# One tile of constants made 32 bytes longer in a two-layer hybrid decoder trunk

## Chip, cores and metric

The kernel runs on one core of a Trainium2 chip. The metric is the device time of one execution in microseconds (us), the median of several runs; lower is better.

## The reference

Two layers of a post-norm decoder trunk over 256 tokens of width 1024, all in float32. For each layer:

```
proj = x @ w_in                       # 1024 -> 12800, cut into the parts below
y_A  = B * conv3_causal(C * h)        # short gated convolution, width 1024
y_B  = dilated attention, 3 groups of 8 heads of 64 (window, dilation) = (128,1), (512,4), (2048,16),
       rotary on q and k, the groups merged by their softmax denominators
y_C  = gelu(u) * (tril(W_s) @ LN(gelu(v)) + b)      # per chunk of 128 tokens, width 1024
m = sig(g_A)*(y_A P_A) + sig(g_B)*(y_B P_B) + sig(g_C)*(y_C P_C)
x = LN(alpha*x + m W_o)
x = LN(alpha*x + (silu(x W_gate) * (x W_up)) W_down)   # inner width 2816
```

## The kernel before

Every large product is made of three matmuls. A float32 matrix is split into a high and a low part of 12 bits each (`split`, lines 177 to 180: ScalarE copies the high part, VectorE subtracts it), kept in the type fp32r, 4 bytes an element, and h.T h' + h.T l' + l.T h' is summed in PSUM. Weights come from HBM in panels (`Panel`, line 144), three of them in flight (tile `raw`, 8 KB a partition), and are split in pieces of 512 columns just before TensorE needs them. `tick` (line 209) puts this work of the other engines, and attention, between runs of matmuls; it goes by a planned TensorE time that `spend` adds up (327 ns for three matmuls of 256 columns, 1.28 ns a column for three of 512).

There are two forms of the large product:

- `feat` (line 250, matmuls on lines 246 to 248): features on partitions. Weights of 128 columns stand, 256 tokens move. The moving tile is xh or xl (the two parts of x, with features on partitions), or the parts of a branch: yah, yal (convolution), ybh, ybl (attention), ych, ycl (gMLP). A panel has 48 matmuls (24 for the attention branch).
- `toks` (line 263, matmuls on lines 266 to 268): tokens on partitions. 128 tokens of x (xh, xl), of the hidden units of the feed-forward (hh, hl) or of the summed branches (mh, ml) stand, and the weights move, 512 columns at a time, or 256 in the first two blocks of the feed-forward.

In the names of the trace the moving tile comes first: `acc<-xh,wh` moves xh against standing weights wh, `acc<-wh,hh` moves weights against standing hidden units.

The rest of TensorE's work is small: transposes by an identity that is kept in the constants `con` (lines 296, 442, 451, 612, 804), the scores and the products with values of attention (lines 591 to 595, 622), and the gMLP's spatial product (line 701, plain fp32; one such matmul is two instructions).

Places in the SBUF, per partition. A tile begins at the next multiple of 32 bytes behind the one before. The constants come first: `con` (line 130) has 1282 columns of 4 bytes, 5128 bytes, and begins at byte 16512, a multiple of 64. Behind it, in this order: xt at 21664, xh at 29856, xl at 38048, cos, sin, two small constants, the three `raw` tiles from 48352 in steps of 8192, and the 72 slots (`flat`, line 110) from 72928 in steps of 2048, which hold split weights, branches, hidden units, queries, keys and everything else of that size. Small tiles follow. All of xt, xh, xl, raw and the slots so begin at 32 past a multiple of 64; xh and xl at 32 past a multiple of 128, the slots at 96 past one. Rows of 1024 or 2048 bytes within them are what a matmul reads, and begin in the same manner.

Of the kernel before, what the change touches and what calls it, by code (L numbers as in the profile page):

```python
# [11 lines left out]
F32 = mybir.dt.float32  # L12
# [26 lines left out]

# Weights: columns split at a time, panels loaded ahead.  # L40
PIECE = 512
RAW = 3
# Slots of 2 KB a partition; those that weights leave to others.
NS = 72
SPARE = 8
# TensorE time between two turns of the other engines' work, ns.
TICK = 1300
# Pieces of weights to have ready for splits to wait behind a layer norm.
CALM = 8
# [3 lines left out]
WAIT = 5  # L53
# Steps of attention a turn.
PACE = 0.5

# Column layout of the constants.
C_ID = 0
# [4 lines left out]
C_N = C_M + 2 * 512  # L63

TWO_PI = 2 * math.pi
# Pieces, of few bits each, of 2*pi and of (2**20, 2**9)/(2*pi) less its whole turns.
PI_PARTS = (6.283203125, -1.7818063497543335e-05, 2.4308402678243113e-10)
# [5 lines left out]
def constants():  # L73
    """Identity, masks and rotary frequencies: they depend on shapes alone."""
    c = np.zeros((128, C_N), np.float32)
    i = np.arange(128)
    c[:, C_ID:C_ID + 128] = np.eye(128)
    # Attention keeps tokens ordered by their residue mod 2, in two tiles: a tile of queries sees
    # all keys of the first group, and of the dilated ones only the keys of its own tile.
    tok = np.arange(S).reshape(128, 2).T.reshape(-1)  # L80
    for t in range(2):
        own = slice(t * 128, (t + 1) * 128)
        m = C_M + t * 512
        for g, (keys, n) in enumerate(((slice(0, S), S), (own, 128), (own, 128))):
            dist = tok[own, None] - tok[None, keys]
            ok = (dist >= 0) & (dist % DIL[g] == 0) & (dist <= 128 * DIL[g])
            c[:, m:m + n] = np.where(ok, 0.0, NEG)
            m += n
    c[:, C_TRI:C_TRI + 128] = i[:, None] <= i[None, :]
    c[:, C_FREQ] = (10000.0 ** (-(i % 32) / 32.0)).astype(np.float32)  # L90
    c[:, C_SGN] = np.where(i % 64 < 32, -1.0, 1.0)
    return c
# [3 lines left out]
def trunk(ctx: ExitStack, tc: tile.TileContext, a, out):  # L96
# [32 lines left out]

    con = cp.tile([128, C_N], F32, name="con")  # L130
    ident = con[:, C_ID:C_ID + 128]
# [7 lines left out]

    # ---------------------------------------------------------------- weights  # L140
    cnt = dict(loaded=0, split=0, made=0, front=0, hold=4, calm=0)
    panels = []

    class Panel:
        """Weights [kc * 128, nw], kept as 12-bit parts h + l in pieces of 512 columns."""

# [22 lines left out]
        def at(self, k, c, n):  # L169
            """Columns c..c+n of row block k, both parts."""  # L170
            i, o = divmod(k * self.nw + c, PIECE)
            while len(self.h) <= i:
                piece()
            cnt["front"] = max(cnt["front"], self.first + i + 1)
            return self.h[i][:, o:o + n], self.l[i][:, o:o + n]

    def split(h, l, src):
        """h + l = src, both of them of 12 bits."""
        nc.scalar.activation(h, src, AF.Copy)  # L179
        V.tensor_tensor(l, src, h.bitcast(F32), op=OP.subtract)  # L180
# [15 lines left out]
    def used(n=1):  # L196
        """Pieces of weights done with."""
        free(2 * n)
# [6 lines left out]
    def soon(n, f):  # L205
        """f at the n-th turn from here."""
        timed.append((clock[1] + n, f))

    def tick():
        """Work of other engines, and attention, between runs of matmuls."""  # L210
        clock[1] += 1
        loaded = False
        while timed and timed[0][0] <= clock[1]:
            timed.pop(0)[1]()
            loaded = True
        if hooks:
            hooks.popleft()()
        clock[2] += PACE if slow else 0
        if clock[2] >= 1:
            clock[2] -= 1  # L220
            slow.popleft()()
            loaded = True
        lead = cnt["made"] - cnt["front"]
        if clock[1] <= cnt["calm"] and lead >= CALM:
            n = 0
        elif lead < LOW:
            n = 2
        elif loaded:
            n = 1 if lead < HIGH else 0
        elif slow:  # L230
            n = 2 if lead < TOP else 1
        else:
            n = 1 + (clock[1] % 2 and not hooks)
        for _ in range(n):
            if cnt["made"] != cnt["hold"] and cnt["split"] < len(panels) and live[0] + 2 + SPARE <= NS:
                piece()
# [7 lines left out]
    def mm3(o, hl, rhs_h, rhs_l, first, last):  # L244
        """o (+)= h.T @ (h' + l') + l.T @ h'."""
        nc.tensor.matmul(o, lhsT=hl[0], rhs=rhs_h, start=first, stop=False)  # L246
        nc.tensor.matmul(o, lhsT=hl[0], rhs=rhs_l, start=False, stop=False)  # L247
        nc.tensor.matmul(o, lhsT=hl[1], rhs=rhs_h, start=False, stop=last)  # L248

    def feat(p, rhs):  # L250
        """Features on partitions: (panel).T @ activations, a bank for two blocks."""
        ps = acc()
# [10 lines left out]
    def toks(ps, lhs, p, k, c, n, first, last):  # L263
        """Tokens on partitions: activations.T @ panel, one row block into one bank."""
        h, l = p.at(k, c, n)
# [9 lines left out]
    def by_residue(x):  # L275
        """Tokens (innermost) in the order of attention."""
        if len(x.shape) == 2:
# [14 lines left out]
    def to_features(t, q):  # L292
        """Half of x of a token tile, transposed and split."""
        ps = trp()
# [4 lines left out]

    # ---------------------------------------------------------------- layer norm  # L300
    def load_gb(g, b, dma=nc.gpsimd.dma_start):
# [8 lines left out]
    def norm(src, stats, gb, done=lambda h: None):  # L310
        """Layer norm in place of rows of 1024: src the halves, stats their bn_stats."""
        mv = small("mv", (128, 2))
# [6 lines left out]
        V.reciprocal(sd[:, 1:2], sd[:, 0:1])  # L319
        # One Newton step: y (1.5 - 0.5 (v + eps) y y).  # L320
        V.scalar_tensor_tensor(sd[:, 2:3], sd[:, 1:2], sd[:, 3:4], sd[:, 1:2], op0=OP.mult, op1=OP.mult)
# [13 lines left out]
    def resid(t, h, ps):  # L335
        """x = alpha x + (a branch), and the statistics of the half row."""
        V.scalar_tensor_tensor(x_half(t, h), x_half(t, h), ALPHA, ps, op0=OP.mult, op1=OP.add)  # L337
# [3 lines left out]

    # ---------------------------------------------------------------- rotary tables
    rope = {}
# [5 lines left out]
    def rope_tables():  # L349
        """sin and cos of position * frequency, exactly reduced for any position."""  # L350
        pos = rope["pos"]
# [55 lines left out]

    # ---------------------------------------------------------------- one layer
    def layer(L, steps):
# [9 lines left out]

        # Small parameters of the layer.  # L420
        def params():
# [38 lines left out]

        # gMLP gate: gelu and layer norm, tokens on partitions.
        v_t = {}
# [45 lines left out]
        c = OFF_V  # L508
        steps.append(([win(c + nh * 512, 512, 4, k0) for nh in range(2) for k0 in (0, 4)], gv))

        # Attention values, tokens on partitions.
        va = {}
# [17 lines left out]

        # Queries and keys, rotated; features on partitions.
        qk = {}

        def stack(hf, w, r):
            """12-bit parts of the first group: a product over 128 rows gives both cross terms of a head."""
            up, dn = slice(0, 64), slice(64, 128)
# [4 lines left out]
            for i, (own, other) in enumerate(((up, dn), (dn, up))):  # L541
                s = slot("stack", F32R)
                if w:
                    # k: low part at the head's own rows, high part at the others.
                    nc.scalar.activation(s[other], r[own], AF.Copy)
                    V.tensor_tensor(s[own], r[own], kh[own].bitcast(F32), op=OP.subtract)
                else:
                    # q: high part at the head's own rows, low part at the others.
                    nc.scalar.activation(s[own], r[own], AF.Copy)
# [29 lines left out]
        def attend(hf):  # L579
            """Queue attention of four heads behind the next panels."""  # L580
            state = {}
# [74 lines left out]

        # Short convolution.
        ya = {}
# [31 lines left out]

        # gMLP: u * (tril(W_s) v + b).
        yc = {}
# [28 lines left out]

        # Gates, branch products, their sum.
        mT = {}
# [36 lines left out]

        # x = LN(alpha x + m W_o)
        def wo(P):
# [16 lines left out]

        # Feed-forward.  # L780
        hT = {}

        def ff_first(P):
            """The first two blocks: tokens on partitions, a token tile at a time."""
            for j in range(2):
# [109 lines left out]

    # TensorE's clock rises with use: keep it busy until the data arrives.
    idle = small("idle", (128, 64), 1)
# [45 lines left out]
```

## Time and profile before

| | us |
|---|---|
| median of 3 runs | 1177.97 (1177.68 to 1178.27) |
| span of the profiled execution | 1174.9 |
| TensorE busy in it | 1164.0 |
| VectorE busy | 789.3 |
| ScalarE busy | 622.8 |

The profiled execution has no time of its own beside its span, from the first to the last instruction; the runs' times contain some work around it. How to read it: each engine has its own queue, so an engine's busy time counts only where nothing else ends later. Matmuls are pipelined: the next begins before the one before has ended, so the duration of one (some 280 ns for 256 columns) is longer than the distance from its start to that of the next, and the sum of durations exceeds the busy time. A timeline gives each matmul's start, and so this distance.

### The profile page before, as it was taken

What the parts mean: (1) busy time and instruction counts of PE and PEld (TensorE: products, weight loads), DVE (VectorE), ACT (ScalarE), POOL (GpSimd) and SP (SyncE); (2) the same over time, 40 slices, a digit from 0 to 9 for tenths busy, and PEclk for the clock granted to TensorE, in tenths of its full rate; (3) what the DMA queues carried; (4) which work ended last, traced back from release to release, by engine and by line L of the source; (5) the groups of instructions that cost most, each with busy time, mean ns of one, the idle gap of its engine ahead of it and who ended that gap; (6) DMA issues with size and microseconds to landing.
All of it is one profiled execution on the core that took longest, in us unless ns stands there. A gap on an engine that the chain in (4) does not pass through costs nothing.

```text
span 1174.9 us, 21651 instructions
## 1 busy us (share of the span) xinstructions
PE 1164.0 (99%) x8884; PEld 1101.0 (94%) x8884; DVE 789.3 (67%) x1426; ACT 622.8 (53%) x1126; POOL 14.2 (1%) x29
## 2 busy tenths in 40 slices
PE   9999999999999999999999999999999999999997
PEld 7899999999999899998888999999999999999985
DVE  6978886666755777556496677766676567764534
ACT  6666554676544466445185454546755444654530
POOL 0000000000000000000100000000000000000000
PEclk9999999999999999999999999999999999999999
DMA  9588554435857378448367664453566583774530
GB/s 343 202 258 251 171 167 146 142 126 197 265 178 235 111 228 281 171 146 317 113 215 250 181 188 135 151 172 109 177 216 204 194 251 108 253 234 160 176 111 36
DMA packets 180695, 222.41 MB, mean 189 GB/s; under 512 B 5456, under 2 KB 154228, under 8 KB 180596
## 3 DMA queue, kind: packets, MB, share of 16 engines
q1 hardware_dynamic: 178500, 214.66, 55.7%
q0 software_dynamic: 1952, 6.31, 1.9%
q8 instruction: 69, 1.13, 0.4%
q14 instruction: 30, 0.25, 0.1%
q10 hardware_dynamic: 144, 0.07, 0.0%
HBM read 213.67 MB, written 1.05 MB: 183 GB/s over the span
## 4 chain that ended last, share of the span: by engine, by line
PE 98%; DVE 1%; DMA 0%; ACT 0%; SPq 0%; issue 0%
PE acc L246 22%; PE acc L247 21%; PE acc L248 21%; PE acc L267 9%; PE acc L268 9%; PE acc L266 9%; PE acc L622 1%; PE trp L595 1%; PE trp L612 1%; PE trp L592 1%; PE acc L701 1%; PE trp L296 0%; DMA raw<-in_w_in 0%; PE trp L591 0%; PE trp L804 0%; PE trp L442 0%
## 5 line engine op out<-in xcount | busy, mean ns | idle before, releaser
L180 DVE TENSOR_TENSOR wl<-raw,wh 128x512 fp32r<-128x512 f32 x776 | 490.9, 686 | 179.8 <-ACT wh L179 171.2
L246 PE MATMUL acc<-xh,wh 128*128 128x256 f32 x1856 | 523.1, 282 | 0.0
L247 PE MATMUL acc<-xl,wh 128*128 128x256 f32 x1856 | 514.9, 277 | 0.0
L248 PE MATMUL acc<-xh,wl 128*128 128x256 f32 x1856 | 514.8, 277 | 0.0
L179 ACT ACTIVATE wh<-raw 128x512 fp32r<-128x512 f32 x776 | 432.1, 622 | 69.7 <-DMA raw<-in_w_in 26.5
L246 PEld LDWEIGHTS acc<-xh,wh 128*128 128x128 f32 x1856 | 348.8, 188 | 6.0 <-issue 2.1
L248 PEld LDWEIGHTS acc<-xh,wl 128*128 128x128 f32 x1856 | 349.8, 188 | 0.0
L247 PEld LDWEIGHTS acc<-xl,wh 128*128 128x128 f32 x1856 | 348.8, 188 | 0.1
L266 PE MATMUL acc<-wh,xh 128*128 128x512 f32 (+1 forms) x288 | 100.4, 349 | 0.3 <-ACT xh L179 0.3
L267 PE MATMUL acc<-wl,xh 128*128 128x512 f32 (+1 forms) x288 | 98.8, 343 | 0.2 <-DVE wl L180 0.2
L268 PE MATMUL acc<-wh,xl 128*128 128x512 f32 (+1 forms) x288 | 98.8, 343 | 0.0
L266 PE MATMUL acc<-wh,hh 128*128 128x512 f32 x176 | 68.6, 390 | 0.0
L268 PE MATMUL acc<-wh,hl 128*128 128x512 f32 x176 | 68.5, 389 | 0.0
L267 PE MATMUL acc<-wl,hh 128*128 128x512 f32 x176 | 68.5, 389 | 0.0
L266 PEld LDWEIGHTS acc<-wh,xh 128*128 128x128 f32 x288 | 54.7, 190 | 7.2 <-ACT wh L179 0.5
L267 PEld LDWEIGHTS acc<-wl,xh 128*128 128x128 f32 x288 | 54.8, 190 | 6.8 <-DVE wl L180 0.5
L268 PEld LDWEIGHTS acc<-wh,xl 128*128 128x128 f32 x288 | 54.7, 190 | 6.6 <-DVE xl L180 0.4
L599 ACT ACTIVATE p<-p,ml 128x512 f32<-128x512 f32 x32 | 23.3, 728 | 61.3 <-DVE ml L598 56.3
L179 ACT ACTIVATE hh<-hs 128x512 fp32r<-128x512 f32 x18 | 11.4, 634 | 64.3 <-DVE hs L823 64.3
L316 ACT ACTIVATE sd<-mv,eps 128x1 f32<-128x1 f32 x12 | 3.6, 298 | 72.4 <-DVE mv L313 72.4
L337 DVE SCALAR_TENSOR_TENSOR xt<-xt,acc 128x512 f32<-128x512 f32 x16 | 11.0, 685 | 44.5 <-PE acc L268 44.5
L268 PEld LDWEIGHTS acc<-wh,hl 128*128 128x128 f32 x176 | 33.0, 188 | 6.8
(148 smaller groups left out, 1329.1 us busy)
## 6 DMA issues: line engine op xcount, KB each, us to landing
raw<-in_w_in SPq DMA_DIRECT2D x99, 1024.0 KB, 5.3
raw<-in_w_gate SPq DMA_DIRECT2D x22, 1024.0 KB, 5.8
raw<-in_w_up SPq DMA_DIRECT2D x22, 1024.0 KB, 5.2
raw<-in_w_down SPq DMA_DIRECT2D x22, 1024.0 KB, 4.8
raw<-in_p_a SPq DMA_DIRECT2D x8, 1024.0 KB, 5.3
raw<-in_p_c SPq DMA_DIRECT2D x8, 1024.0 KB, 5.1
raw<-in_w_o SPq DMA_DIRECT2D x8, 1024.0 KB, 5.7
sw<-qk SPq DMA_DIRECT2D x96, 64.0 KB, 3.0
```

Of the source, the lines that this page charges most:

```text
L179: nc.scalar.activation(h, src, AF.Copy)
L180: V.tensor_tensor(l, src, h.bitcast(F32), op=OP.subtract)
L246: nc.tensor.matmul(o, lhsT=hl[0], rhs=rhs_h, start=first, stop=False)
L247: nc.tensor.matmul(o, lhsT=hl[0], rhs=rhs_l, start=False, stop=False)
L248: nc.tensor.matmul(o, lhsT=hl[1], rhs=rhs_h, start=False, stop=last)
L266: nc.tensor.matmul(ps, lhsT=lhs[0], rhs=h, start=first, stop=False)
L267: nc.tensor.matmul(ps, lhsT=lhs[0], rhs=l, start=False, stop=False)
L268: nc.tensor.matmul(ps, lhsT=lhs[1], rhs=h, start=False, stop=last)
L592: nc.tensor.matmul(ps[:, c], lhsT=q[d, b, own], rhs=qk[hf, "kh"][d, b, keys], start=False, stop=True)
L595: nc.tensor.matmul(ps[:, c], lhsT=q[d, b, own], rhs=k[d, b, keys], start=True, stop=True)
L599: nc.scalar.activation(p, p, AF.Exp, bias=ml[:, 0:1], scale=-1.0, accum_out=ml[:, 1:2])
L612: nc.tensor.transpose(ps[:, i * 128:(i + 1) * 128], p[:, i * 128:(i + 1) * 128], ident)
```

## The change

The tile of the constants is allocated with 8 more columns, 32 bytes, of which nothing is used. Its place and the columns that are read stay. Every tile behind it begins 32 bytes later: xh at 29888, xl at 38080, the slots from 72960. The distances between those tiles stay. Apart from that the change takes comments and descriptions out of the file and leaves empty lines in their place, so that line numbers are the same; the hunks that do only this are left out here.

```diff
@@ -127,7 +127,7 @@
     def trp():
         return pt.tile([128, 512], F32, tag="trp", name="trp")
 
-    con = cp.tile([128, C_N], F32, name="con")
+    con = cp.tile([128, C_N + 8], F32, name="con")[:, :C_N]
     ident = con[:, C_ID:C_ID + 128]
     xt = cp.tile([128, 2, D], F32, name="xt")
     xh = cp.tile([128, 8, S], F32R, name="xh")
```

## Rows read from the trace of the kernel before

**Rows 1.** The page: span; busy time; TensorE's granted clock; the last chain.
```profile
span 1174.9 us, 21651 instructions
...
PE 1164.0 (99%) x8884; PEld 1101.0 (94%) x8884; DVE 789.3 (67%) x1426; ACT 622.8 (53%) x1126; POOL 14.2 (1%) x29
...
PEclk9999999999999999999999999999999999999999
...
PE 98%; DVE 1%; DMA 0%; ACT 0%; SPq 0%; issue 0%
```

**Rows 2.** Waits of TensorE, longest first: total us, times, longest us.
```profile
PE trp L905 <- DVE half_pi L900: 1.0, 1, 1.0
```

**Rows 3.** TensorE's groups by line and shape: count, busy us, mean ns of one.
```profile
L246 PE MATMUL acc<-xh,wh 128*128 128x256 f32 x1856 | 523.1, 282 | 0.0
...
L266 PE MATMUL acc<-wh,hh 128*128 128x512 f32 x176 | 68.6, 390 | 0.0
...
L266 PE MATMUL acc<-wh,xh 128*128 128x512 f32 x160 | 63.8, 399 | 0.3 <-ACT xh L179 0.3
...
L266 PE MATMUL acc<-wh,xh 128*128 128x256 f32 x128 | 36.5, 286 | 0.0
L246 PE MATMUL acc<-yah,wh 128*128 128x256 f32 x128 | 36.5, 285 | 0.0
...
L266 PE MATMUL acc<-wh,mh 128*128 128x512 f32 x64 | 25.3, 395 | 0.0
...
L612 PE MATMUL trp<-con,p 128*128 128x128 f32 x128 | 19.2, 272 | 0.0
L246 PE MATMUL acc<-ybh,wh 128*128 128x256 f32 x64 | 18.3, 286 | 0.0
...
L701 PE MATMUL acc<-wsT,gv 128*128 128x128 f32 x64 | 8.4, 274 | 0.0
```

**Rows 4.** Timeline of TensorE, feed-forward of layer 0: start us, us; first and last of 831.
```profile
430.79 0.28 PE L246 MATMUL acc<-xh,wh 128*128 128x256 f32 x1
...
524.86 0.28 PE L248 MATMUL acc<-xh,wl 128*128 128x256 f32 x1
```

**Rows 5.** The same timeline, feed-forward of layer 1: first and last of 828.
```profile
1008.64 0.28 PE L246 MATMUL acc<-xh,wh 128*128 128x256 f32 x1
...
1106.04 0.28 PE L248 MATMUL acc<-xh,wl 128*128 128x256 f32 x1
```

**Rows 6.** The same timeline, branch products of layer 0: first and last of 111.
```profile
305.29 0.28 PE L246 MATMUL acc<-yah,wh 128*128 128x256 f32 x1
...
318.49 0.28 PE L248 MATMUL acc<-ych,wl 128*128 128x256 f32 x1
```

**Rows 7.** The same timeline, down projection of layer 1: first and last of 261.
```profile
1106.15 0.39 PE L266 MATMUL acc<-wh,hh 128*128 128x512 f32 x1
...
1165.09 0.39 PE L268 MATMUL acc<-wh,hl 128*128 128x512 f32 x1
```

**Rows 8.** The same timeline, first products of layer 0: two stretches, 75 and 141.
```profile
13.39 0.39 PE L266 MATMUL acc<-wh,xh 128*128 128x512 f32 x1
...
30.33 0.39 PE L268 MATMUL acc<-wh,xl 128*128 128x512 f32 x1
...
31.25 0.40 PE L266 MATMUL acc<-wh,xh 128*128 128x512 f32 x1
...
63.91 0.40 PE L268 MATMUL acc<-wh,xl 128*128 128x512 f32 x1
```

**Rows 9.** The same timeline: a transpose of attention, and the gMLP's spatial product.
```profile
130.00 0.60 PE L612 MATMUL trp<-con,p 128*128 128x128 f32 x4
...
219.54 1.05 PE L701 MATMUL acc<-wsT,gv 128*128 128x128 f32 x8
```

**Rows 10.** The page: groups of the weights' split on VectorE and ScalarE.
```profile
L180 DVE TENSOR_TENSOR wl<-raw,wh 128x512 fp32r<-128x512 f32 x776 | 490.9, 686 | 179.8 <-ACT wh L179 171.2
...
L179 ACT ACTIVATE wh<-raw 128x512 fp32r<-128x512 f32 x776 | 432.1, 622 | 69.7 <-DMA raw<-in_w_in 26.5
```

## The prediction

> **What bounds the kernel now.** I read the page first, for the engine that sets the end: TensorE is busy for 99% of the span, its granted clock is full in every slice, and the chain that ended last is 98% TensorE and 1% VectorE [rows 1]. Second, the waits of TensorE: the longest in the whole trace is 1.0 us, at the start [rows 2]. So no load, split or wait sets the time; only the rate at which TensorE passes from one matmul to the next does. Third, therefore, the timeline of TensorE, where the reader should look at the distance between the starts of neighbouring matmuls (the pitch), not at the duration of one, since durations overlap. I take a long unbroken stretch, subtract its first start from its last and divide by the number of steps.
>
> - xh or xl moving (256 columns), weights standing: 430.79 to 524.86 us holds 831 matmuls, so 94.07 us / 830 = 113.3 ns [rows 4]. The same code in the second layer, 1008.64 to 1106.04 us, 828 matmuls: 97.40 / 827 = 117.8 ns [rows 5].
> - a branch (slots) moving, 256 columns, weights standing: 305.29 to 318.49 us, 111 matmuls: 13.20 / 110 = 120.0 ns [rows 6].
> - weights moving, 512 columns, hidden units (slots) standing: 1106.15 to 1165.09 us, 261 matmuls: 58.94 / 260 = 226.7 ns [rows 7].
> - weights moving, 512 columns, x standing: 13.39 to 30.33 us, 75 matmuls: 16.94 / 74 = 228.9 ns; then 31.25 to 63.91 us, 141 matmuls: 32.66 / 140 = 233.3 ns [rows 8].
> - the identity in con moving (a transpose, 128 columns, which take as long as 256 of the others): four in 0.60 us, of which the last takes 0.272 us, so 0.328 / 3 = 109 ns [rows 9, 3]. A plain fp32 product of 128 columns out of a slot: eight in 1.05 us, (1.05 - 0.274) / 7 = 111 ns [rows 9, 3].
>
> At 2.4 GHz a column takes 0.4167 ns, so 256 take 106.7 and 512 take 213.3 ns. Every fp32r pitch is over that, and by an odd kind of amount. In units of 16 columns (6.67 ns) the pitches are 17.0, 17.67 (53 per three matmuls), 18.0, 34.0, 34.33 and 35.0, where 16 and 32 would be enough. Sixteen columns of 4 bytes are 64 bytes. That is how a reader looks that fetches its moving operand in aligned pieces of 64 bytes, at the speed at which it uses them up: a row of 1024 bytes that begins 32 past a multiple of 64 touches 17 pieces instead of 16. The one tile that begins at a multiple of 64, con, is the one with 109 ns and no whole piece on top. This is an inference: con's matmuls are transposes, so they differ from the others in more than the place. The fp32 product out of a slot, at 111 ns, reads half as many bytes in that time and is hardly held up either, which fits a limit on bytes fetched.
>
> **The change part by part.** It adds no instruction, no DMA and no wait, and moves none: only addresses change, by 32 bytes, for all tiles behind con. Unchanged are the distances between these tiles. Comments fall away, which costs nothing.
>
> Counts are of [rows 3]: a group of L246 stands for three lines, L246 to L248, a group of L266 for L266 to L268.
>
> Forecast: one piece of 64 bytes less in each fp32r matmul, 6.67 ns, but none faster than con's 109 ns.
> 1. xh moving: 3 x 1856 = 5568. The stretch of rows 5 (828) at 6.67 ns: 5.5 us. The other 4740 I count at 113.3, though shorter stretches of 117.8 lie among them: 113.3 to 109 is 4.3 ns, 20.6 us. Together 26.1.
> 2. branches moving: 3 x (128 + 128 + 64) = 960 (ych has as many as yah), 6.67 ns: 6.4.
> 3. weights moving, slots standing: 3 x (176 + 64) = 720: 4.8.
> 4. weights moving in 512 columns, x standing: 3 x 160 = 480: 3.2.
> 5. weights moving in 256 columns, x standing: 3 x 128 = 384. They have no pitch of their own here; taken as 113.3, 4.3 ns: 1.7.
> Sum 42.2 us.
>
> Lower end: all of them go to con's rate, columns plus 109 - 106.7 = 2.3 ns, so 109 and an estimate of 215.7 ns. Then 1: 20.6 + 828 x 8.8 = 27.9; 2: 960 x 11.0 = 10.6; 3: 720 x 11.0 = 7.9; 4: a third at 13.2, two thirds at 17.6: 7.7; 5: 1.7. Sum 55.8 us. I take the single piece, since what is over it (18 for 17, 34 for 33, 35 for 33) differs between pairs of operands that are misplaced alike, so something other than the place makes it.
>
> First what the rows show: 113.3 to 120 ns for 256 columns and 226.7 to 233.3 for 512. Beside it stands the Trainium skill, TensorE: Matmul & The Clock Gate, section "Wait — 56ns, not 53.3ns?": warm matmuls start N/2.4 ns plus about 2.5 ns apart, which would be 109.2 and 215.8. The trace agrees for con's transposes (109) and not for the fp32r matmuls; if the change brought them there, the sum would be that of the lower end.
>
> **What covers it.** A panel of 48 matmuls falls from 5.4 to 5.2 us. In it VectorE needs 4 x 686 ns and ScalarE 4 x 622 ns for its splits [rows 10], 2.7 and 2.5 us; so neither becomes the bound, and I cost the shift at nothing there. If alignment alters VectorE's own operations, what shows is the 1% of the chain that it holds, 12 us: even 5% of them, either way, is 0.6 us. DMAs write to shifted rows too; no DMA stands in the chain (0%) [rows 1], so a faster one brings nothing, and a slower one would have to use up the panels that are loaded ahead. Zero, with 0.6 us of room.
>
> **The rivals.**
> - *Only the tiles in slots gain* (terms 2 to 5, 16.1 us: 1161.9). In bytes modulo 128, xh begins at 32 and slots at 96; after the change at 64 and 0. If whole pieces are fetched from a multiple of 128 on, the counts would be (32 + 1024)/64, up to 17, for xh, (96 + 1024)/64, up to 18, for the branches and (96 + 2048)/64, up to 34, for the hidden units: exactly rows 4, 6 and 7. Then xh at 64 stays at 17. Against it: weights moving with x standing begin at 96 too, and take 34.33 and 35 [rows 8].
> - *No change* (1178.0): the extra 16 columns come of how the weight load and the moving stream take turns, which hangs on the distance between their tiles, and that stays. For it: rows 4, 6 and 8 differ at the same misplacement modulo 64, and one code has two pitches [rows 4, 5]. Against it: what is left over is always a multiple of a third of a piece or a whole one, and con has nearly none. Also here: a reader with pieces of 32 bytes or less, for which these tiles are in place already. The Trainium skill, SBUF — State Buffer, section "Specifications (TRN2)", speaks for this one: it gives cachelines of 16 bytes, so the shift would do nothing. No row here shows pieces of 16 bytes; the steps seen are of 64.
> - *Slower*: the two pitches of rows 4 and 5 are two ways in which the same two streams lock, and a stretch keeps the one that it fell into. A shift of 32 bytes can set which one it falls into. If the slower one takes hold of the other 4740 matmuls of xh, that is 4740 x (117.8 - 113.3) = 21 us: 1199. It decides from the point where more than about half of them are caught and the shift saves no piece.
> - That the change does not do what it says: con is 5128 bytes, kept in 5152 as places go in steps of 32; 5160 need 5184, so the tiles do move. I give this nothing.
>
> **How the numbers follow.** The profiled execution has a span of 1174.9 us [rows 1], 3.1 below the median of 1177.97; I keep that distance. Forecast: 1177.97 - 42.2 = 1135.8 (span 1132.7), chance 0.33. To con's rate: 1122.2, 0.20. Only slots: 1161.9, 0.10. No change: 1178, 0.22. Slower: 1199, 0.15. So faster by over 0.2% has 0.63, within 0.2% (2.4 us, about what a measurement of this kernel can tell from no change) 0.22, slower 0.15. The range goes from 1119, the lower end with some room for the shorter stretches that I counted as fast, to 1181, which takes in no change; it leaves out the slower case, 0.15.
>
> **What would show it.** Right: con's transposes stay at 109 ns; the xh stretch of 430 to 525 us shows 109 to 111 ns; the branches 113.3 or less, the hidden units 220 or less; instruction counts, the clock and the shares of the chain stay. If xh stays at 113.3 while the branches go to 113.3 or less, it is the reader from multiples of 128. If every pitch of the first list stands as it was, the pieces are no matter of the place. I am wrong as well if pitches fall but TensorE begins to wait for splits: then the waits of TensorE, 1.0 us at most now, would grow.

## The result, and the profile after

The changed kernel takes 1183.93 us against 1178.12 of the kernel before on the same chip: 1.0051 times as long, 95% interval 1.0036 to 1.0065. It is slower by 5.8 us. The page of the kernel after, in the parts that [rows 1] shows of before:

```profile
span 1181.1 us, 21651 instructions
...
PE 1170.6 (99%) x8884; PEld 1107.5 (94%) x8884; DVE 789.6 (67%) x1426; ACT 621.7 (53%) x1126; POOL 14.2 (1%) x29
...
PEclk9999999999999999999999999999999999999999
...
PE 99%; DVE 1%; DMA 0%; SPq 0%; issue 0%; ACT 0%; DVEq 0%
```

TensorE is still the bound, and the whole loss is in its busy time (1164.0 to 1170.6 us) at a full clock, with the same number of instructions. The waits of TensorE, longest first, have not grown beside [rows 2]:

```profile
PE trp L905 <- DVE half_pi L900: 1.0, 1, 1.0
```

So the pitch has to be read again. The timeline of TensorE in the kernel after (start us, us, line), first and last matmul of the feed-forward of layer 0 (834 matmuls, [rows 4]), of layer 1 (828, [rows 5]), of a block of branch products (111, [rows 6]) and of the down projection (261, [rows 7]):

```profile
430.80 0.28 PE L246 MATMUL acc<-xh,wh 128*128 128x256 f32 x1
...
528.91 0.28 PE L248 MATMUL acc<-xh,wl 128*128 128x256 f32 x1
...
1014.85 0.28 PE L246 MATMUL acc<-xh,wh 128*128 128x256 f32 x1
...
1112.25 0.28 PE L248 MATMUL acc<-xh,wl 128*128 128x256 f32 x1
...
305.46 0.28 PE L246 MATMUL acc<-yah,wh 128*128 128x256 f32 x1
...
318.66 0.28 PE L248 MATMUL acc<-ych,wl 128*128 128x256 f32 x1
...
1112.37 0.39 PE L266 MATMUL acc<-wh,hh 128*128 128x512 f32 x1
...
1171.30 0.39 PE L268 MATMUL acc<-wh,hl 128*128 128x512 f32 x1
```

Layer 1: 97.40 / 827 = 117.8 ns; branches: 13.20 / 110 = 120.0; hidden units: 58.93 / 260 = 226.7. All three are to the digit what they were. But layer 0: 98.11 / 833 = 117.8 ns, where [rows 4] had 113.3. A second long stretch did the same: the first rotated panels of layer 1. First and last of 441 matmuls, in the kernel before (49.87 / 440 = 113.3 ns):

```profile
643.53 0.28 PE L246 MATMUL acc<-xh,wh 128*128 128x256 f32 x1
...
693.40 0.28 PE L248 MATMUL acc<-xh,wl 128*128 128x256 f32 x1
```

and in the kernel after (51.82 / 440 = 117.8 ns):

```profile
647.74 0.28 PE L246 MATMUL acc<-xh,wh 128*128 128x256 f32 x1
...
699.56 0.28 PE L248 MATMUL acc<-xh,wl 128*128 128x256 f32 x1
```

No pitch here is new. xh moving against weights has two steady pitches, 340.0 and 353.3 ns for three matmuls (a triple: lines 246, 247 and 248 once), and the change moved stretches from the one to the other. I counted triples of such matmuls with no other work between them, from the starts in the two traces: before, 1,255 at 340 ns, the pitch of [rows 4], and 423 at 353.3 ns, that of [rows 5]; after, 823 and 857 (the stretches above hold 278, 276 and 147 of them). The 434 more at 13.33 ns make 5.79 us, and 5.81 were lost between the medians. The two profiled spans lie 6.2 us apart; 0.3 us of that is in the 384 matmuls that move 256 weight columns past x, 45.8 us from each start to the next before and 46.1 after, because more of them stand 118 ns apart.

The rows that the prediction leaned on as the one aligned tile, con, and as the plain fp32 product out of a slot ([rows 9]), after:

```profile
130.11 0.60 PE L612 MATMUL trp<-con,p 128*128 128x128 f32 x4
...
219.67 1.05 PE L701 MATMUL acc<-wsT,gv 128*128 128x128 f32 x8
```

Both are as long as before, though the slot now begins at a multiple of 64 like con. So it was not their place that set con's transposes apart. They are transposes of 128 columns in plain float32; which of these makes their 109 ns is not shown.

### The profile page after: what moved, and what is told of

It reads as the page before. It is cut to its first block, busy times and chain, and to the rows that moved or that the text cites. A ratio compares the mean times of both kernels' runs of the same rounds, so it can differ in the third digit from the quotient of the medians.

```text
span 1181.1 us, 21651 instructions
## 1 busy us (share of the span) xinstructions
PE 1170.6 (99%) x8884; PEld 1107.5 (94%) x8884; DVE 789.6 (67%) x1426; ACT 621.7 (53%) x1126; POOL 14.2 (1%) x29
## 4 chain that ended last, share of the span: by engine, by line
PE 99%; DVE 1%; DMA 0%; SPq 0%; issue 0%; ACT 0%; DVEq 0%
PE acc L246 22%; PE acc L248 21%; PE acc L247 21%; PE acc L267 9%; PE acc L266 9%; PE acc L268 9%; PE acc L622 1%; PE trp L595 1%; PE trp L612 1%; PE trp L592 1%; PE acc L701 1%; PE trp L296 0%; DMA raw<-in_w_in 0%; PE trp L591 0%; PE trp L804 0%; PE trp L442 0%
```

## The experiments

All kernels below are the kernel before with the edit shown. "Slow" is a triple of xh matmuls at 353.3 ns, counted as above; a time is the median, a ratio that to the kernel before on the same chip.

**Does the place modulo 64 or 128 make it?** Shifts of 64 and of 128 bytes; the edit for 64:

```diff
-    con = cp.tile([128, C_N], F32, name="con")
+    con = cp.tile([128, C_N + 16], F32, name="con")[:, :C_N]
```

> The constants' tile is 64 bytes longer than before: all later tiles begin at 32 past a multiple of 64 again, as before, but 64 bytes further. Where the time went is known from the two traces: the pitches are the same in both (113.3 and 117.8 ns for xh moving, 120.0 for branches, 226.7 for hidden units), but the slower of the two pitches of xh holds 857 of the triples of matmuls instead of 423, and 434 x 13.3 ns = 5.8 us is the whole difference. Theory 'place': the place modulo 64 decides which pitch a stretch falls into; then this is 1178 us as before, with some 423 slow triples. Theory 'accident': any shift changes the phase in which stretches begin and so draws anew; then it may lie anywhere from 1172 (no slow triple) to 1196 (all slow), and need be neither 1178 nor 1184.

Measured: 1175.26 us, ratio 0.9980 (0.9971 to 0.9988), 262 slow.

> The constants' tile is 128 bytes longer than before: every place modulo 64 and modulo 128 is that of the kernel before. Theory 'place': 1178 us and the same stretches at the slower pitch as before, whether it goes by 64 or by 128. Theory 'accident': a new draw between 1172 and 1196 us.

Measured: 1174.85 us, ratio 0.9982 (0.9973 to 0.9990), 200 slow. The feed-forward of layer 1, first and last of 825:

```profile
1010.78 0.28 PE L246 MATMUL acc<-xh,wh 128*128 128x256 f32 x1
...
1104.17 0.28 PE L248 MATMUL acc<-xh,wl 128*128 128x256 f32 x1
```

93.39 / 824 = 113.3 ns, where the kernel before had 117.8 [rows 5], with every place the same modulo 128. Neither a place modulo 64 nor one modulo 128 decides.

**Is it chance, then?** Each kernel was profiled a second time.

> The kernel before, profiled a second time. Of 1,686 triples of xh against weights that no other work interrupts, 1,255 had 340 ns and 423 had 353.3 ns in its first trace. Theory 'fixed': which pitch a stretch falls into is set by the program (its order, its places), so the same stretches are slow again and the count is 423 to within some ten. Theory 'chance': it is drawn anew in every execution; then the counts differ by whole stretches (147 and 277 triples), and the times of one kernel would scatter by 2 to 4 us.

Measured: 422 slow, in the same stretches.

> The changed kernel, profiled a second time: 823 triples at 340 ns and 857 at 353.3 ns in its first trace. Theory 'fixed': the same long stretches are slow (the feed-forward of both layers, 277 and 276 triples, and the first rotated panels of layer 1, 147). Theory 'chance': other ones are.

Measured: 857 slow again. I cut the xh matmuls at every interruption into 95 stretches and called each by its more frequent pitch: between the two traces of the kernel before none of 95 differs, between those of the changed kernel 2; between the kernel before and the changed one 20. As far as two executions of each show, it is fixed by the program, theory "fixed".

**By which place?** Shifts of 256 and of 2048 bytes.

> The constants' tile is 256 bytes longer than before: places modulo 64, 128 and 256 are those of the kernel before. The run with 128 bytes more had the same places modulo 128 and yet another set of slow stretches (200 slow triples against 423, the feed-forward of layer 1 fast). Theory 'place modulo 256': the set of the kernel before comes back, 423 slow triples to within some ten. Theory 'any shift': a new set, any number between about 150 and 1,686.

> The constants' tile is 2048 bytes longer than before: every place modulo 2048 is that of the kernel before, and every slot stands where the next one stood. Theory 'place modulo up to 2048': the set of the kernel before, 423 slow triples. Theory 'any shift': a new set, any number between about 150 and 1,686.

Measured: 422 and 423 slow, with none of the 95 stretches different from the kernel before in either. The feed-forward of layer 1 with 2048 bytes, first and last of 828, is slow again (97.40 / 827 = 117.8 ns), as in [rows 5]:

```profile
1008.66 0.28 PE L246 MATMUL acc<-xh,wh 128*128 128x256 f32 x1
...
1106.06 0.28 PE L248 MATMUL acc<-xh,wl 128*128 128x256 f32 x1
```

So the set goes by the place modulo 256, as far as one execution of each shows, and from the place of the kernel before alone; the other places were not tried again 256 bytes further on. The tiles can stand at eight such places in steps of 32; the four not yet run:

> The constants' tile is 96 bytes longer: all later tiles at a multiple of 64, as in the changed kernel, but 64 bytes further. So far the slow triples of xh are 423 with no shift, 857 with 32, 262 with 64, 200 with 128, and again 422 and 423 with 256 and 2048 bytes. Theory 'multiples of 64': a place at a multiple of 64 makes the slower pitch hold on; then this has some 850 slow triples and about 1183 us. Theory 'place modulo 256': each of the eight places has a set of its own, and nothing but chance makes that of 32 large; then this may be anything from 150 up, and of the four places at a multiple of 64 (shifts 32, 96, 160, 224) some are as fast as the others.

> Shift of 160 bytes, at a multiple of 64. Theory 'multiples of 64': some 850 slow triples, about 1183 us. Theory 'place modulo 256': a set of its own.

> Shift of 192 bytes, at 32 past a multiple of 64, the fourth such place modulo 256. Theory 'multiples of 64': 200 to 423 slow triples, as the other three of its kind (423, 262, 200), 1175 to 1178 us. Theory 'place modulo 256': a set of its own.

> Shift of 224 bytes, at a multiple of 64. Theory 'multiples of 64': some 850 slow triples, about 1183 us. Theory 'place modulo 256': a set of its own.

Measured, all eight, with the span of the profiled execution (one of each):

| shift, bytes | place modulo 64 | slow triples | span, us | span less 13.33 ns each |
|---|---|---|---|---|
| 0 (before) | 32 | 423 | 1174.9 | 1169.3 |
| 32 (after) | 0 | 857 | 1181.1 | 1169.7 |
| 64 | 32 | 262 | 1173.0 | 1169.5 |
| 96 | 0 | 259 | 1173.4 | 1169.9 |
| 128 | 32 | 200 | 1173.0 | 1170.3 |
| 160 | 0 | 756 | 1179.7 | 1169.6 |
| 192 | 32 | 246 | 1174.2 | 1170.9 |
| 224 | 0 | 444 | 1176.7 | 1170.8 |

The last column is what the time would be with no slow triple; it is the same within 1.6 us for all, while executions of the kernel before alone lie between 1174.5 and 1178.1 us. With 96 bytes the tiles stand at multiples of 64 and the span is as short as with 64 or 128. Theory "multiples of 64" falls as a rule, though the two worst places are of that kind. How a place makes its set is open; what the traces say of it stands behind the next experiment.

**Is the pitch a state that the work ahead leaves behind?** Behind all six blocks of branch products xh runs at 113.3 ns in both kernels. So six matmuls of that sort (a slot against a slot) were added in four places, to both kernels:

```diff
+    def lock(p):
+        h, _ = p.at(0, 0, 256)
+        ps = trp()
+        for _ in range(6):
+            nc.tensor.matmul(ps[:, :256], lhsT=h[:, :128], rhs=h, start=True, stop=True)
...
         def rot(hf, g, w):
             def f(P):
+                if hf == g == w == 0:
+                    lock(P[0])
                 ps = feat(P[0], xf)
...
         def ff_gate(j):
             def f(P):
+                if j == 3:
+                    lock(P[0])
                 ps = feat(P[0], xf)
```

> The kernel before, with six added matmuls (a piece of weights against itself, 256 columns, into a spare bank that nobody reads) in four places: ahead of the first rotated panel and of the gate panel j = 3, in each layer. They move a slot's tile against a slot's tile, distance 0 modulo 128, as the branch products do; behind all six blocks of branch products in both traces xh ran at 113.3 ns. Theory 'lock': the pitch of a stretch is a state of the two read streams that whatever came just before leaves behind; then all long stretches behind the added matmuls run at 113.3 ns, the feed-forward of layer 1 too (277 triples x 13.3 = 3.7 us gained), against 24 x 0.12 = 2.9 us for the added work: 1177 us, and about 150 slow triples. Theory 'place': the tiles' places make the pitch; then the feed-forward of layer 1 stays at 117.8 ns and the time rises by 2.9 us to 1180.5.

> The changed kernel with the same added matmuls. Theory 'lock': the three long slow stretches (277, 276 and 147 triples) go to 113.3 ns, 700 x 13.3 = 9.3 us gained against 2.9 us of added work: 1177.5 us, equal to the kernel before with the same matmuls within 1.5 us, so the places modulo 64 cost nothing by themselves. Theory 'place': 1186.5 us, 2.9 more than the changed kernel, and those stretches stay at 117.8 ns.

Measured: the kernel before with them 1178.29 us (1.0006, 0.9998 to 1.0015), 281 slow; the changed one with them 1177.47 us (1.0002, 0.9993 to 1.0011), 176 slow. The timeline of the former around the added matmuls in layer 1:

```profile
1019.74 0.28 PE L248 MATMUL acc<-xh,wl 128*128 128x256 f32 x1
...
1020.80 0.28 PE L248 MATMUL acc<-xh,wl 128*128 128x256 f32 x1
1020.92 0.88 PE L276 MATMUL trp<-wh 128*128 128x256 f32 x6
...
1021.99 0.28 PE L246 MATMUL acc<-xh,wh 128*128 128x256 f32 x1
...
1108.58 0.28 PE L248 MATMUL acc<-xh,wl 128*128 128x256 f32 x1
```

Ahead of them nine matmuls in 1.06 us, 117.8 ns; behind them 765 at 86.59 / 764 = 113.3 ns. Same tiles, same places: the pitch is a state. This takes the 5.8 us out of the change: with the three long stretches reset, the changed kernel is no slower than the kernel before. In the kernel before the gain of 3.4 us (255 triples) was eaten by the added work, 2.9 us, and by another stretch (82 to 119 us, 105 triples) that now fell to the slower pitch.

The eight traces of the table show the state without any added work, and where the place may come in. Of the stretches between two interruptions, 89 have at least one undisturbed triple of xh. Behind attention scores (32 stretches) and branch products (6), where slots move against slots at distance 0 modulo 256, all are at 113.3 ns at every place. Behind a product with values (line 622, 12) or the spatial product (line 701, 2) each stretch is at the other pitch than the stretch ahead of it, at every place: this work hands the state on, and it too reads slots against slots, so distance 0 alone does not reset it. Behind transposes with con, 30 of 33 stretches change with the place. And con is the one tile here that no shift moves. So in these runs the place modulo 256 is the same as the distance of the shifted tiles to con, and no run tells the two apart. Of the four stretches left, behind weights that move past x at a distance that stays, three change as well.

**What sets the two pitches?** Shifting only raw and the slots against x, by 32 and 64 bytes; the edit for 32:

```diff
-    half_pi = cp.tile([128, 1], F32, name="half_pi")
+    half_pi = cp.tile([128, 9], F32, name="half_pi")[:, :1]
```

> Constants as before, but the tile half_pi is 32 bytes longer: x's tiles (xt, xh, xl) stay, raw and the slots move by 32 bytes, so the distance between a moving xh and standing weights is 32 modulo 128 instead of 64. Theory 'distance': the pitch hangs on the distance between the moving and the standing tile modulo 128 (0 for branches against weights: 18 units of 16 columns; 64 for xh against weights: 17 or 17.67); then xh gets a pitch that neither kernel shows, branches (distance 0 still) stay at 120.0 ns and hidden units at 226.7. Theory 'kind': the distance doesn't matter, branches are slower for another reason; then xh stays at 113.3 and 117.8 ns, and the time between 1172 and 1196 us.

> As the run before, with 64 bytes: xh stays at 32 past a multiple of 128, the slots come to 32 as well, distance 0 modulo 128. Theory 'distance': xh moving goes to 18 units, 120.0 ns, as branches have it; over the 1,768 triples without an interruption, of which 1,255 are at 340 and 423 at 353.3 ns before, that is about 1255 x 20 + 423 x 6.7 ns = 28 us, so 1206 us. Theory 'kind': 1172 to 1196 us, xh at 113.3 and 117.8 ns.

Measured: 1196.47 us (1.0163, 1.0150 to 1.0176) and 1200.34 us (1.0197, 1.0184 to 1.0210). The feed-forward of layer 1 with 64 bytes, first and last of 828:

```profile
1031.60 0.28 PE L246 MATMUL acc<-xh,wh 128*128 128x256 f32 x1
...
1129.74 0.28 PE L248 MATMUL acc<-xh,wl 128*128 128x256 f32 x1
```

98.14 / 827 = 118.7 ns. Over the whole trace uninterrupted xh matmuls come to 117.8 ns on the mean with 32 bytes and 118.7 with 64, against 114.6 before; branches, whose distance to the weights did not change, stay at 119.9 in both, hidden units at 227. It is not the places by themselves: x stands where it stands in the kernel before, the slots where the shifts of con by 32 and 64 bytes put them, and in those runs xh has 113.3 and 117.8 ns alone. The distance between the moving and the standing tile sets which pitches there are. The pitch with 64 bytes is not the 120 of the branches, though the distance is 0 modulo 128 for both: modulo 256 it is 128 for xh and 0 for branches. To test that, 68 slots of 2176 bytes instead of 72 of 2048, 8.5 times 256, whose distance alternates between 0 and 128 modulo 256, without and with the branches' parts set 64 bytes into their slots:

```diff
-        return sl.tile([128, 512], dt, tag="slot", name=name)
+        return sl.tile([128, 544], dt, tag="slot", name=name)[:, off:off + 512]
...
-                        yb[hf] = (slot(f"ybh{hf}", F32R), slot(f"ybl{hf}", F32R))
+                        yb[hf] = (slot(f"ybh{hf}", F32R, 16), slot(f"ybl{hf}", F32R, 16))
```

> Control for the next run: 68 slots of 2176 bytes instead of 72 of 2048, of which 128 bytes are left unused, so all places modulo 128 and the distances modulo 128 stay as before; the order of the work is the same. Theory 'distance': branches stay at 120.0 ns (18 units), hidden units at 226.7, xh at 113.3 and 117.8 in a set of its own: 1173 to 1196 us.

> As the run before, and the parts of the branches (ya, yb, yc) begin 64 bytes into their slots, so their distance to the weights against which they move is 64 modulo 128 instead of 0. Theory 'distance': the branches go from 18 units to 17 or 17.67, 120.0 to 113.3 or 117.8 ns; 291 steady triples x 20 ns = 5.8 us at the faster one, 1.9 at the slower one, against the run before, apart from the set of slow stretches of xh, which is counted in both. Theory 'kind': branches stay at 120.0 ns.

Measured: 1177.27 us (0.9996, 0.9987 to 1.0005) and 1176.10 us (0.9987, 0.9977 to 0.9996). The control failed as a control: it moved the branches from 119.8 to 118.2 ns and the hidden units from 227 to 231.5, so modulo 128 is not enough. With the 64 bytes the branches came to 117.1. 66 slots of 2304 bytes, 9 x 256, again with the branches' 64 bytes, keep one distance for all:

> 66 slots of 2304 bytes (a multiple of 256, so that all slots have one place modulo 256), and the branches' parts 64 bytes into theirs: distance to the weights 64 modulo 256 throughout, with xh, weights and hidden units at the places of the kernel before. In the run with slots of 2176 bytes the distance alternated between 64 and 192 and the branches came to 17.55 units on the mean. Theory 'distance modulo 256': branches at 17 units, 113.3 ns, or 17.67 where they lock so; 291 steady triples x 20 ns = 5.8 us less, hidden units stay at 226.7 ns, and xh keeps the set of the kernel before (423 slow triples) up to the branches: about 1172 us. Theory 'no more than the mean of 64 and 192': branches 17.5, 2.6 us less: 1175.

Measured: 1176.17 us (0.9989, 0.9981 to 0.9998). Hidden units are back at 227 ns. Branches of layer 0, first and last of 120, 14.02 / 119 = 117.8 ns instead of 120.0 [rows 6]:

```profile
335.98 0.28 PE L246 MATMUL acc<-yah,wh 128*128 128x256 f32 x1
...
350.00 0.28 PE L248 MATMUL acc<-ych,wl 128*128 128x256 f32 x1
```

With a distance as far from 0 as that of xh (64 against 192 modulo 256), branches have xh's two pitches: 46 triples at 340.0 and 261 at 353.3 ns. Most fell into the slower one. And they no longer set xh right behind them: two of the six stretches there are slow throughout, and there are 518 slow triples in all instead of 423.

> The same with the constants' tile 128 bytes longer, the place with the fewest slow triples among the eight (200 against 423). By 'distance' and 'place modulo 256' both gains add up: 5.8 + 3.0 us, about 1169 us, unless the branches' new pitch draws the stretches behind them anew.

Measured: 1184.30 us (1.0060, 1.0048 to 1.0072), 1,036 slow, and 306 of the branches' triples at 353.3 ns. The gains did not add up: all six stretches behind branch products are now slow, 188 of the 518 more slow triples, and the feed-forward of layer 0, another 276. This also serves as a control for the added matmuls, for the same branch products, moved away from distance 0, interrupt xh as before and no longer set its pitch. Added matmuls at another distance were not run.

The fastest versions are the shifts of 64 and 128 bytes, by 0.2% against the kernel before. The two with the branches' 64 bytes and con in place gain 0.1%, and the single runs with 96 and 192 bytes, 1175.22 and 1175.96 us against 1178.08, lie about where those with 64 and 128 do.

## Why the prediction was wrong, point by point

- **What bounds the kernel** was right: TensorE's pitch, at a full clock, with no wait, and this is where the whole loss lies.
- **One piece of 64 bytes less in each matmul**, all five terms, 42.2 us: none of it came. The pitches of xh, branches and hidden units at a multiple of 64 are those at 32 past one, and weights moving past x gained nothing either (term 5 went 0.3 us the other way). The step that failed is the one from pitches "in units of 16 columns" to a reader that "fetches its moving operand in aligned pieces of 64 bytes". The units are there, but the extra ones hang on how the moving tile lies to the standing one: 113.3 or 117.8, 120.0, and means of 117.8 and 118.7 ns at four distances. The prediction had the sign of this in hand, 17 and 18 at the same misplacement modulo 64 ([rows 4] and [rows 6]), and put it aside as a remainder.
- **The lower end by con** fell with it: con's 109 ns does not come of its place, for the fp32 product takes its 111 ns out of a slot at either place, and the fp32r matmuls keep their pitches at a multiple of 64. Nor did the change bring the fp32r matmuls to the N/2.4 + 2.5 ns of the Trainium skill, TensorE: Matmul & The Clock Gate, section "Wait — 56ns, not 53.3ns?": 113.3 and 117.8 ns stand against 109.2, an estimate from its formula for 256 columns. That con's 109 ns agrees with it holds only if the 128 float32 columns of a transpose are counted as 256, as the prediction did.
- **Only the tiles in slots gain**: wrong. With slots at a multiple of 128 the hidden units still take 34 units and the branches 18.
- **No change** was right that the pitches hang on the distance between the tiles, which stays (shown by the shifted slots), and wrong that nothing else follows. That the weight load and the moving stream take turns is not shown.
- **Slower** had the mechanism: two states at one distance, kept along a stretch, of which a shift sets the one. The shifts and the added matmuls show it; that the states are two ways in which streams lock is not shown. Its size was wrong: it counted all 4,740 matmuls of xh outside [rows 5] as caught, 21 us, where 434 triples, 1,302 matmuls, were, 5.8 us. So its time was 15 us too high, and its point of decision, half of them, was wrong too, as a good quarter was enough. Given 0.15, it lay outside the range; had each long stretch been taken as a draw of its own, the case would have begun right above 1178, and the range would have had to take it in.
- **What covers it**: the shift cost the other engines nothing, as forecast. The split on VectorE takes 686 ns as before, the busy times are 789.6 and 621.7 us, and the waits did not move. Whether the splits would keep up with shorter panels was not put to the test, since no panel became shorter.

## What to carry to other kernels

Where TensorE is the bound, take the pitch from the starts, stretch by stretch, and look whether one piece of code has two of them: then a change of nothing but addresses can be worth from 0.2% less to 0.5% more time, as here, and a small measured gain of another edit may be only this. The distance between moving and standing tile, modulo 256 bytes, is worth 2 to 6% of a matmul's pitch here and can be set by a few bytes of padding. But look at both forms of the product: distance 0 is the slow one for 256 moving columns (120.0 ns) and the fast one for 512 (226.7 ns, against 228.9 and 233.3 with x standing). A regularity in sizes (all pitches in units of 16 columns) tells a grain, but not whose: before it is made a forecast of 40 us, look for two rows that share the supposed cause and differ in the effect.

## What the runs showed of the hardware

- fp32r matmuls with 256 columns and weights loaded for each have steady pitches of 17, 17.67 or 18 units of 16 columns (113.3, 117.8, 120.0 ns), none of them 16, at any of the eight places. Why not 16 was not found.
- By distance of the moving to the standing tile modulo 256, for 256 columns: 0 gives 120.0 ns (branches), 64 and 192 give 113.3 or 117.8, 128 and 160 give means of 118.7 and 117.8 (xh with shifted slots). At 512 columns 0 gives 226.7 ns (hidden units standing), 64 gives 228.9 to 233.3 (x standing), and slots whose distance alternates between 0 and 128 give a mean of 231.5.
- The choice between 113.3 and 117.8 is kept over hundreds of matmuls, returned in a second execution of both kernels, and came back with a shift of 256 or 2048 bytes. It was 113.3 behind the six added matmuls at distance 0 in all eight places (four in each of two kernels), in six of which it is 117.8 without them. What keeps it no run shows, and how the place modulo 256 enters is open; the distance to con, which stays put, is the nearest candidate.
